# Output gates of two mixers, with tokens in rows and ahead of the transposition

## The chip, the cores and the metric

The kernel runs on one core of a Trainium2 chip. The metric is the device time of one launch in microseconds (us); the time of a kernel is the median over its runs. The engines that matter here: TensorE (PE) multiplies matrices, VectorE (DVE) and ScalarE (ACT) work elementwise, GpSimd (POOL) computes the few reciprocal roots of the norms, and SyncE (SP) issues the transfers from memory. Each engine works through its own queue in order.

## The reference

Two layers of a block for 256 tokens of 2048 columns, in float32. A projection `w_in` gives the inputs of three mixers: a convolution over time, HGRN (a gated linear recurrence, 6 heads of 128) and retention (6 heads of 128). HGRN and retention normalize the output of each head and multiply it with a gate from the same projection. That part, cut to what the change touches:

```python
# hgrn2_mixer, o: (b, t, heads, 128)
o = o * lax.rsqrt(jnp.mean(jnp.square(o), axis=-1, keepdims=True) + LN_EPS)
return o.reshape(b, t, D_HGRN) * norm_g * jax.nn.sigmoid(g_in.astype(jnp.float32))
# retention_mixer
o = ((o - mu) * lax.rsqrt(var + LN_EPS)).reshape(b, t, D_RET) * gn_g + gn_b
return jax.nn.silu(g_in.astype(jnp.float32)) * o
# the layer
mix = jnp.concatenate([y_conv, y_hgrn, y_ret], axis=-1).astype(dtype)
h = jnp.einsum('bte,ed->btd', mix, w_out[l])
x = layer_norm(DEEPNORM_ALPHA * x + h, ln1_g[l], ln1_b[l]).astype(dtype)
```

Behind it come a feed-forward part (2048 to 8192 to 2048, squared ReLU) and a second layer norm.

## The kernel before

**Matmuls.** Each float32 weight is split into two parts, by ScalarE (`hi`, L289) and VectorE (`lo`, L292), and so is each activation, and a product is three matmuls of parts. A unit of weights is 128 x 1024; units go through three raw buffers and six split ones (`wp`). There are two forms:

- `xstat` (matmuls in `mmx`, L315): the activation is the stationary operand. A group gives 256 tokens x 512 columns with tokens in rows, as 96 matmuls of 512 columns, 12 to a unit of weights.
- `wstat` (L366 and L368): the weights are the stationary operand. A call gives 256 columns (one pair of heads) with tokens along the free side, as 2 blocks of 16 pairs of matmuls, one 512 and one 256 wide, 8 pairs to a unit. Each block is evicted by a ScalarE copy (L375) and a VectorE sum (L378).

**The mixer stage of a layer.** `ORDER` lists the `wstat` calls. Three `xstat` groups `vgroup` give the values of HGRN and retention, the first ahead of the list, the others before ("hf", 2) and ("rq", 0). `hgrn` and `ret` do one pair of heads: TensorE computes scores in small float32 matmuls (HGRN: a diagonal, L591, and seven levels, L607, between which VectorE multiplies decays into both sides, L626 and L631; retention: L720, L721), then `out_heads` (L551 to L555) gives the heads' output with tokens in rows. VectorE takes the statistics (L530, L532), GpSimd the root, ScalarE scales (L667, L764), TensorE transposes (`transpose4`, L402), and only then, with channels in partitions, come the norm's factors (`hng`, `rgg`, `rgb`, a scalar for each partition), the gate from `wstat` (kinds "hg" and "rg"), and the split into `mixT` by `split_act` (L391, L393). The output projection `wo`, four `xstat` groups, reads `mixT`; the last quarter of its inputs are retention's pairs 1 and 2.

**What sets the order.** A planner (`Plan`) takes every operation with a cost and its dependences, and writes each engine's instructions in order of its own modelled times; TensorE's large matmuls (`main`) keep the program's order, the small ones and the other engines' work are put between them. The order is fixed when the program is built. Buffers come from rings: `r2` (11 of 128 x 512), `r1` (4 of 128 x 256), `mm` and `aux` (4 PSUM banks each).

Of the kernel before, what the change touches and what calls it, by code (L numbers as in the profile page):

```python
# [28 lines left out]
HP = 3  # L29


ORDER = [("cg", 0), ("ca", 0), ("hf", 0), ("hq", 0), ("hg", 0), ("cg", 1), ("ca", 1),
         ("hf", 1), ("hq", 1), ("hg", 1), ("hf", 2), ("hq", 2), ("hg", 2),
         ("rq", 0), ("rk", 0), ("rg", 0), ("rq", 1), ("rk", 1), ("rq", 2), ("rk", 2),
         ("rg", 1), ("rg", 2)]

MIXK = ((4, 8), (0, 4), (12, 4))
MT = (2, 0, 1, 3)
# [162 lines left out]
def block_kernel(ctx: ExitStack, tc: tile.TileContext, a: dict, out: bass.AP):  # L201
# [24 lines left out]
    def act(n, ptr=0, ps=False):  # L226
        return 0.000833 * n + (0.051 if ps else 0.093) + 0.093 * ptr
# [11 lines left out]
        C[name_] = cst.t[:, o_:o_ + n_]  # L239
        o_ += n_  # L240
    ident, tri = C["ident"], C["tri"]
    hng = C["hng"].rearrange("p (l n) -> p l n", l=2)
    rgg = C["rgg"].rearrange("p (l n) -> p l n", l=2)
    rgb = C["rgb"].rearrange("p (l n) -> p l n", l=2)
    clg = C["clg"].rearrange("p (l n) -> p l n", l=2)
    clb = C["clb"].rearrange("p (l n) -> p l n", l=2)
    cbd = C["cbd"].rearrange("p (l n) -> p l n", l=2)
# [149 lines left out]
    def transpose4(src, r, **kw):  # L397
        pt = aux.buf()

        def fn():  # L400
            for i in range(4):
                nc.tensor.transpose(out=pt.t[:, i * P:(i + 1) * P], in_=src()[:, i * P:(i + 1) * P], identity=ident)  # L402
# [138 lines left out]
    def out_heads(units, r, vt, col0):  # L541
# [16 lines left out]
        op("PE", 6 * 0.216, fn, r=r + vb, w=[po])  # L558
        return po

    def hgrn_gates(l, p, pr, pair):

        Tt, Kt = pv(pair, 0), pv(pair, 1)
        op("ACT", act(W), lambda: S.activation(out=Tt(), in_=pr.t, func=AF.Sigmoid), r=[pr], w=[(pair, "T")])
        op("ACT", act(W), lambda: S.activation(out=Kt(), in_=pr.t, func=AF.Sigmoid, scale=-1.0), r=[pr],
           w=[(pair, "K")])
        if l:
            for h in range(2):
                c = 2 * p + h
# [13 lines left out]
    def hgrn(l, p, pair, gate, vt, mixT):  # L583
# [78 lines left out]
        op("POOL", POW, lambda: rsqrt(s.t[:, 32:36], s.t, 40, 4), r=[mhalf], w=[s])  # L662
        on = r2.buf()

        def scale():
            for b in range(4):
                S.activation(out=on.t[:, b * P:(b + 1) * P], in_=po.t[:, b * P:(b + 1) * P], func=AF.Copy,  # L667
                             scale=s.t[:, 40 + b:41 + b])

        op("ACT", 4 * act(P, 1, True), scale, r=[po, s], w=[on])  # L670
        pt = transpose4(lambda: on.t, [on, cst])
        y = r2.buf()

        def gated():
            for h in range(2):
                c, sl = 2 * p + h, slice(h * T, (h + 1) * T)
                V.scalar_tensor_tensor(out=y.t[:, sl], in0=pt.t[:, sl], scalar=hng[:, l, c:c + 1],
                                       in1=gate.t[:, sl], op0=ALU.mult, op1=ALU.mult)
# [29 lines left out]
    def ret(l, p, pair, gate, vt, mixT):  # L708
# [59 lines left out]
        pt = transpose4(lambda: on.t, [on, cst])
        y = r2.buf()

        def affine():
            for h in range(2):
                c, sl = 2 * p + h, slice(h * T, (h + 1) * T)
                S.activation(out=y.t[:, sl], in_=pt.t[:, sl], func=AF.Identity, scale=rgg[:, l, c:c + 1],
                             bias=rgb[:, l, c:c + 1])

        op("ACT", 2 * act(T, 2, True), affine, r=[pt, cst], w=[y])
        op("DVE", dve(W), lambda: V.tensor_tensor(out=y.t, in0=y.t, in1=gate.t, op=ALU.mult), r=[gate], w=[y])
        blk = 10 + 2 * p
        mt, o = mixT[MT[blk // 4]], blk % 4  # L780
        split_act(mt, slice(o, o + 2), slice(0, T), lambda: y.t, [y], ("o", o))
# [167 lines left out]
    for l in range(DEPTH):  # L949
# [22 lines left out]
        else:  # L972
            vgroup(0, head=HEAD)
            norm.rest()
        pairs, gates = {}, {}
        for i, (kind, p) in enumerate(ORDER):
            if (kind, p) == ("hf", 2):
                vgroup(1)
            if (kind, p) == ("rq", 0):
                vgroup(2)  # L980
            if kind in ("hf", "rq"):
                pair = pairbufs.buf()
                pairs[kind[0], p] = pair
            dst = None
            if kind in ("rq", "rk"):
                dst = (pairs["r", p], "Q" if kind == "rq" else "K", pv(pairs["r", p], 0 if kind == "rq" else 1))
            pr = wstat(a["wp"][l, i], xT, dst)
            if l == 0 and i == 1:
                op("DMA", 6.0, lambda: nc.sync.dma_start(out=x_nat.t, in_=a["x"].rearrange("(t p) d -> p t d", p=P)),
                   w=[x_nat], after=(plan.last["PE"],))  # L990
            if kind == "hf":
                hgrn_gates(l, p, pr, pair)
            elif kind == "hq":
                Qv = pv(pair, 2)
                op("ACT", act(W), lambda Qv=Qv, pr=pr: S.activation(out=Qv(), in_=pr.t, func=AF.Sigmoid), r=[pr],
                   w=[(pair, "Q")])
                op("DVE", dve(W), lambda Qv=Qv, pr=pr: V.tensor_tensor(out=Qv(), in0=pr.t, in1=Qv(), op=ALU.mult),
                   r=[pr], w=[(pair, "Q")])
            elif kind == "hg":
                gate = r2.buf()  # L1000
                op("ACT", act(W), lambda gate=gate, pr=pr: S.activation(out=gate.t, in_=pr.t, func=AF.Sigmoid),
                   r=[pr], w=[gate])
                hgrn(l, p, pairs["h", p], gate, vt, mixT)
            elif kind in ("cg", "ca"):
# [15 lines left out]
            elif kind == "rg":  # L1020
                gate = r2.buf()
                op("ACT", act(W), lambda gate=gate, pr=pr: S.activation(out=gate.t, in_=pr.t, func=AF.Sigmoid),
                   r=[pr], w=[gate])
                op("DVE", dve(W), lambda gate=gate, pr=pr: V.tensor_tensor(out=gate.t, in0=pr.t, in1=gate.t,
                                                                           op=ALU.mult), r=[pr], w=[gate])
                ret(l, p, pairs["r", p], gate, vt, mixT)
# [76 lines left out]
def _columns():  # L1103

    start, off = {}, 0
    for name, n in (("ca", 512), ("cg", 512), ("hq", 768), ("hf", 768), ("hi", 768), ("hg", 768),
                    ("rq", 768), ("rk", 768), ("rv", 768), ("rg", 768)):
        start[name] = off
        off += n
    v = np.concatenate([start["hi"] + np.arange(768), start["rv"] + np.arange(768)])  # L1110
    blocks = []
    for kind, p in ORDER:
        base = start[kind] + 256 * p
        blocks.append(base + np.arange(256))
    return v, np.concatenate(blocks)
# [65 lines left out]
```

## Time and profile before

| | us |
|---|---|
| median of 3 runs | 2332.24 |
| lowest and highest run | 2331.98, 2335.85 |
| the profiled execution | 2335.01 |
| its span | 2333.2 |

Where layer 0's mixer stage lies in the span: TensorE starts its first stationary-weight stage at 33.2 us and the output projection at 363.9 us; layer 1's output projection starts at 1521.9 us. The granted TensorE clock was 0.998 over the run. In the profile's answers a group of instructions is named by line, engine, operation, and output<-input by the names in the program without buffer numbers; a row of the chain of waits is the start, the length, and what. The rows themselves stand in the prediction.

### The profile page before, as it was taken

To read this page: it belongs to the slowest core of one execution; us is meant where nothing else is said; L and a number is where in the kernel's file an instruction comes from. 1 tells how busy PE (TensorE), PEld (TensorE's weight loads), DVE (VectorE), ACT (ScalarE), POOL (GpSimd) and SP (SyncE) were. 2 spreads that over 40 slices of the span, in tenths; PEclk is the share of its full clock that TensorE was granted. 3 is DMA by queue.
4 is the path that set the end of the run, shared out by engine and by line. 5 is a ranking of instruction groups with operands and counts; after the bars stand their busy time and mean duration, and the time that the engine had idled before them with its cause. 6 is when DMAs were issued, how large, how long until landed. Compare 5 with 4: busy or idle time off the path is not lost.

```text
span 2333.2 us, 29611 instructions
## 1 busy us (share of the span) xinstructions
PE 2318.7 (99%) x12067; PEld 1975.0 (85%) x12067; DVE 1502.6 (64%) x2052; ACT 1050.9 (45%) x1334; POOL 47.9 (2%) x60
## 2 busy tenths in 40 slices
PE   9999999999999999999999999999999999999998
PEld 7888888888888888888888888888888888888886
DVE  6998565665565565565679976657655655655655
ACT  6445444454344344344444455444444444443442
POOL 0000000000000000000000000100000000000000
PEclk9999999999999999999999999999999999999999
DMA  8544556465555555556554445564655555555563
GB/s 291 183 169 163 172 194 212 163 208 189 189 189 190 199 181 193 188 189 205 208 173 161 163 163 177 184 219 171 204 192 196 184 194 186 190 188 198 181 230 113
DMA packets 67705, 439.90 MB, mean 189 GB/s; under 512 B 7664, under 2 KB 7920, under 8 KB 16624
## 3 DMA queue, kind: packets, MB, share of 16 engines
q1 hardware_dynamic: 67568, 438.01, 54.7%
q8 instruction: 94, 1.54, 0.2%
q14 instruction: 43, 0.35, 0.0%
HBM read 432.74 MB, written 2.10 MB: 186 GB/s over the span
## 4 chain that ended last, share of the span: by engine, by line
PE 98%; ACT 1%; DVE 0%; DMA 0%; issue 0%; SPq 0%; DVEq 0%
PE mm L315 44%; PE mm L366 33%; PE mm L368 17%; PE aux L607 2%; PE aux L402 1%; DMA raw<-in_wv 0%; DVE wp L292 0%; PE aux L555 0%; ACT act L391 0%; PE aux L553 0%; PE aux L591 0%; PE aux L551 0%; PE aux L720 0%; ACT wp L289 0%; ACT r L916 0%; PE aux L648 0%
## 5 line engine op out<-in xcount | busy, mean ns | idle before, releaser
L292 DVE TENSOR_TENSOR wp<-raw,wp 128x1024 fp32r<-128x1024 f32 (+1 forms) x786 | 957.5, 1221 | 580.3 <-ACT wp L289 578.7
L366 PE MATMUL mm<-act,wp 128*128 128x512 f32 x3328 | 1180.6, 399 | 0.0
L289 ACT CAST wp<-raw 128x1024 fp32r<-128x1024 f32 (+1 forms) x786 | 825.2, 1052 | 771.8 <-PE mm L315 505.1
L315 PE MATMUL mm<-wp,act 128*128 128x512 f32 x4416 | 1019.4, 391 | 3.0 <-ACT wp L289 1.6
L315 PEld LDWEIGHTS mm<-wp,act 128*128 128x128 f32 x4416 | 825.9, 188 | 176.5 <-DVE wp L292 3.7
L368 PE MATMUL mm<-act,wp 128*128 128x256 f32 x3328 | 933.0, 280 | 0.0
L366 PEld LDWEIGHTS mm<-act,wp 128*128 128x128 f32 x3328 | 625.4, 188 | 151.4
L368 PEld LDWEIGHTS mm<-act,wp 128*128 128x128 f32 x3328 | 628.3, 189 | 0.5
L375 ACT COPY r<-mm 128x256 f32<-128x256 f32 x208 | 77.8, 374 | 371.0 <-PE mm L368 370.6
L378 DVE TENSOR_TENSOR r<-mm,r 128x256 f32<-128x256 f32 x184 | 78.0, 424 | 147.0 <-ACT r L375 146.6
L794 DVE SCALAR_TENSOR_TENSOR r<-u_t,cst,r 128x256 f32<-128x256 f32 x240 | 102.2, 480 | 0.0
L410 POOL TENSOR_TENSOR sm<-sm,mhalf 128x4 f32<-128x4 f32 (+1 forms) x24 | 28.3, 1181 | 2275.8 <-DVE sm L876 1611.7
L391 ACT CAST act<-r 128x512 fp32r<-128x512 f32 x82 | 51.7, 631 | 21.6 <-DVE r L1052 16.1
L393 DVE TENSOR_TENSOR act<-r,act 128x512 fp32r<-128x512 f32 x82 | 56.2, 685 | 0.0
L315 PE MATMUL mm<-act,act 128*128 128x512 f32 x192 | 44.8, 389 | 0.0
L607 PEld LDWEIGHTS aux<-pair 128*128 128x128 f32 x336 | 42.4, 191 | 2.6
L943 DVE TENSOR_TENSOR x_nat<-x_nat,mm 128x512 f32<-128x512 f32 x48 | 31.0, 682 | 18.8 <-PE mm L315 18.7
L1052 DVE SCALAR_TENSOR_TENSOR r<-r 128x512 f32<-128x512 f32 x60 | 41.6, 693 | 2.1
L315 PEld LDWEIGHTS mm<-act,act 128*128 128x128 f32 x192 | 36.0, 188 | 7.5
L607 PE MATMUL aux<-pair 128*128 128x64 f32 x336 | 42.0, 267 | 0.0
L941 DVE SCALAR_TENSOR_TENSOR x_nat<-x_nat,mm 128x512 f32<-128x512 f32 x32 | 20.8, 682 | 13.0 <-PE mm L315 13.0
L896 ACT ACTIVATE x_nat<-x_nat,sm 128x512 f32<-128x512 f32 x6 | 4.9, 817 | 48.1 <-POOL sm L416 48.1
(118 smaller groups left out, 576.4 us busy)
## 6 DMA issues: line engine op xcount, KB each, us to landing
raw<-in_w SPq DMA_DIRECT2D x248, 1024.0 KB, 4.8
raw<-in_wp SPq DMA_DIRECT2D x88, 1024.0 KB, 4.8
raw<-in_wo SPq DMA_DIRECT2D x32, 1024.0 KB, 4.8
raw<-in_wv SPq DMA_DIRECT2D x20, 1024.0 KB, 4.8
raw<-in_w1x SPq DMA_DIRECT2D x8, 1024.0 KB, 5.3
raw<-in_wv SPq DMA_DIRECT2D x6, 512.0 KB, 5.9
pair<-pair SPq DMA_DIRECT2D x24, 128.0 KB, 2.3
x_nat<-in_x SPq DMA_DIRECT2D x1, 2048.0 KB, 9.5
```

The costliest lines, as they stand in the source:

```text
L289: S.copy(out=wt()[:, 0, sl], in_=raw.t[:, rs])
L292: V.tensor_tensor(out=wt()[:, 1, sl], in0=raw.t[:, rs], in1=wt()[:, 0, sl].bitcast(F32), op=ALU.subtract)
L315: nc.tensor.matmul(ps.t, lhsT=xT[k // 4].t[:, xs, k % 4, t * P:(t + 1) * P], rhs=w[:, ws, kb, :], start=(k == 0 and n == 0), stop=(k == KB ...
L366: nc.tensor.matmul(pv, lhsT=w[:, 0, kb, :], rhs=xt[:, :, k % 4, :], start=(k == 0), stop=False)
L368: nc.tensor.matmul(pv[:, 0, :], lhsT=w[:, 1, kb, :], rhs=xt[:, 0, k % 4, :], start=False, stop=(k == KB - 1))
L375: S.copy(out=low.t, in_=ps.t[:, T:])
L378: V.tensor_tensor(out=dst[2]()[:, b * T:(b + 1) * T], in0=ps.t[:, 0:T], in1=low.t, op=ALU.add)
L391: op("ACT", act(n, ps=ps), lambda: S.copy(out=x.t[:, 0, blks, cols], in_=bl(src(), nb)), r=r, w=[(x, part)], **kw)
L393: op("DVE", dve(n), lambda: V.tensor_tensor(out=x.t[:, 1, blks, cols], in0=bl(src(), nb), in1=x.t[:, 0, blks, cols].bitcast(F32), op=ALU.s ...
L607: nc.tensor.matmul(ps.t[:, b * 64:(b + 1) * 64], lhsT=Kt()[:, b * P:(b + 1) * P], rhs=rhs, start=True, stop=True)
L794: V.scalar_tensor_tensor(out=d, in0=src, scalar=cw[:, l, b, j:j + 1], in1=d, op0=ALU.mult, op1=ALU.add)
L1052: op("DVE", dve(W), lambda f=f, r=r: V.scalar_tensor_tensor(out=f.t, in0=r.t, scalar=0.0, in1=r.t, op0=ALU.max, op1=ALU.mult), r=[r], w=[f ...
```

## The change

The gates of HGRN and retention leave the `wstat` list. Three `xstat` groups of 512 columns take their place (`out_gates`), each with two pairs of heads: HGRN 0 and 1, HGRN 2 and retention 0, retention 1 and 2. Gates now come with tokens in rows, like the heads' output. ScalarE's sigmoid reads PSUM directly (for retention VectorE multiplies with the gate's input), and the norm's factors, loaded as rows and broadcast to all partitions, are multiplied in on VectorE; for retention there are two products, the gate with the factor and the gate with the offset. HGRN's scaling and gating become one VectorE operation for each 128 columns; retention's scaled output is multiplied with the one product, and the other is added. The transposition comes after that, and `split_act` reads it from PSUM. A pair of heads starts when its projections and its gate have both been put into the program. Arrays of factors in `cst` (36 of 710 columns) fall away.

```diff
-ORDER = [("cg", 0), ("ca", 0), ("hf", 0), ("hq", 0), ("hg", 0), ("cg", 1), ("ca", 1),
-         ("hf", 1), ("hq", 1), ("hg", 1), ("hf", 2), ("hq", 2), ("hg", 2),
-         ("rq", 0), ("rk", 0), ("rg", 0), ("rq", 1), ("rk", 1), ("rq", 2), ("rk", 2),
-         ("rg", 1), ("rg", 2)]
+ORDER = [("cg", 0), ("ca", 0), ("hf", 0), ("hq", 0), ("gates", 0), ("cg", 1), ("ca", 1),
+         ("hf", 1), ("hq", 1), ("hf", 2), ("hq", 2), ("gates", 1),
+         ("rq", 0), ("rk", 0), ("rq", 1), ("rk", 1), ("rq", 2), ("rk", 2), ("gates", 2)]
+
+GATES = ((("h", 0), ("h", 1)), (("h", 2), ("r", 0)), (("r", 1), ("r", 2)))
...
+    def mixed(y, blk, mixT):
+        pt = transpose4(lambda: y.t, [y, cst])
+        mt, o = mixT[MT[blk // 4]], blk % 4
+        split_act(mt, slice(o, o + 2), slice(0, T), lambda: pt.t, [pt], ("o", o), ps=True)
+
+    def out_gates(l, n, xT):
+        res, after = [r2.buf(), r2.buf()], (plan.last["PE"],)
...
+        def done(t, ps):
+            for j, (kind, p) in enumerate(GATES[n]):
+                src = lambda j=j: bl(ps.t[:, j * T:(j + 1) * T], 2)
+                op("ACT", act(T, ps=True), lambda j=j, src=src: S.activation(
+                    out=view(res[j], t), in_=src(), func=AF.Sigmoid), r=[ps], w=[(res[j], t)], floor=1.5)
+                if kind == "r":
+                    op("DVE", dve(T), lambda j=j, src=src: V.tensor_tensor(
+                        out=view(res[j], t), in0=src(), in1=view(res[j], t), op=ALU.mult), r=[ps], w=[(res[j], t)],
+                       floor=1.5)
+
+        xstat(a["wv"][l, 3 + n], xT, done)
+        for j, (kind, p) in enumerate(GATES[n]):
+            rows = []
+            for name in ("hngr",) if kind == "h" else ("rgbr", "rggr"):
+                row = r1.buf()
+                rows.append(row)
+                op("DMA", 0.5, lambda row=row, name=name, p=p: nc.sync.dma_start(
+                    out=row.t, in_=a[name][l, p * T:(p + 1) * T].partition_broadcast(P)), w=[row], after=after)
+            add = None
+            if kind == "r":
+                add = r2.buf()
+
+            for row in rows:
+                dst = add if row is rows[0] and kind == "r" else res[j]
+                op("DVE", dve(W), lambda j=j, row=row, dst=dst: V.tensor_tensor(
+                    out=view(dst), in0=view(res[j]), in1=bl(row.t, 2).unsqueeze(2).broadcast_to([P, 2, 2, P]),
+                    op=ALU.mult), r=[row, res[j]], w=[dst])
+            yield (kind, p), (res[j] if kind == "h" else (res[j], add))
...
-        op("ACT", 4 * act(P, 1, True), scale, r=[po, s], w=[on])
-        pt = transpose4(lambda: on.t, [on, cst])
-        y = r2.buf()
-
-        def gated():
-            for h in range(2):
-                c, sl = 2 * p + h, slice(h * T, (h + 1) * T)
-                V.scalar_tensor_tensor(out=y.t[:, sl], in0=pt.t[:, sl], scalar=hng[:, l, c:c + 1],
+        def gated():
             for b in range(4):
+                sl = slice(b * P, (b + 1) * P)
+                V.scalar_tensor_tensor(out=on.t[:, sl], in0=po.t[:, sl], scalar=s.t[:, 40 + b:41 + b],
                                        in1=gate.t[:, sl], op0=ALU.mult, op1=ALU.mult)
 
-        op("DVE", 2 * dve(T, 1), gated, r=[pt, gate, cst], w=[y])
...
+        op("DVE", 4 * dve(P, 1), gated, r=[po, s, gate], w=[on])
+        mixed(on, 4 + 2 * p, mixT)
...
-        op("ACT", 2 * act(T, 2, True), affine, r=[pt, cst], w=[y])
-        op("DVE", dve(W), lambda: V.tensor_tensor(out=y.t, in0=y.t, in1=gate.t, op=ALU.mult), r=[gate], w=[y])
...
+        for g, o in zip(gate, (ALU.mult, ALU.add)):
+            op("DVE", dve(W), lambda g=g, o=o: V.tensor_tensor(out=on.t, in0=on.t, in1=g.t, op=o), r=[g], w=[on])
+        mixed(on, 10 + 2 * p, mixT)
...
+        def at_work(k, q):
+            ready.append((k, q))
+            if ready.count((k, q)) == 2:
+                (hgrn if k == "h" else ret)(l, q, pairs[k, q], gates[k, q], vt, mixT)
```

The planner's order moves with it. TensorE, layer 0, the scores of the first HGRN pair (`aux`, from `pair_70`): before, a level stands eight pairs of matmuls behind the one ahead of it, in the `wstat` stages that follow the pair's projections. Here the last pairs ahead of a level, and the level.

```order
L366 MATMUL mm_104<-act_74,wp_67 128x512
L368 MATMUL mm_104<-act_74,wp_67 128x256
L366 MATMUL mm_104<-act_74,wp_67 128x512
L368 MATMUL mm_104<-act_74,wp_67 128x256
L607 MATMUL aux_107<-pair_70 128x64 x4
L366 MATMUL mm_104<-act_75,wp_67 128x512
L368 MATMUL mm_104<-act_75,wp_67 128x256
```

Now the diagonal (L633) and the levels (L649) stand in the gates' own `xstat` stage (L313; `mm_103` and `mm_104` are its two halves of the tokens).

```order
L633 MATMUL aux_106<-pair_70 128x128 x4
L313 MATMUL mm_103<-wp_66,act_73 128x512 x6
L313 MATMUL mm_104<-wp_66,act_73 128x512 x6
L313 MATMUL mm_103<-wp_67,act_73 128x512 x6
L649 MATMUL aux_107<-pair_70 128x64 x4
L313 MATMUL mm_104<-wp_67,act_73 128x512 x6
L313 MATMUL mm_103<-wp_68,act_74 128x512 x6
L649 MATMUL aux_108<-pair_70 128x64 x4
```

Between two levels lie twelve `xstat` matmuls where eight pairs lay; five of the seven levels come in this stage, the other two in the `wstat` stage behind it.

TensorE, layer 0, the end of the stage: the last retention pair. Before, its transposition stood twelve pairs ahead of the output projection, in the last gate's stage.

```order
L366 MATMUL mm_102<-act_72,wp_66 128x512
L368 MATMUL mm_102<-act_72,wp_66 128x256
L402 MATMUL aux_106<-cst,r_4_84 128x128 x4
L366 MATMUL mm_102<-act_73,wp_66 128x512
L368 MATMUL mm_102<-act_73,wp_66 128x256
```

Now the transpositions of pairs 1 and 2 (L400) stand inside the first group of the output projection, which reads `act_76`, `act_78`, `act_77` and, for retention's pairs 1 and 2, `act_79`.

```order
L400 MATMUL aux_105<-cst,r_10_90 128x128 x4
L313 MATMUL mm_102<-wp_64,act_78 128x512 x6
L313 MATMUL mm_101<-wp_65,act_78 128x512 x6
L313 MATMUL mm_102<-wp_65,act_78 128x512 x6
L313 MATMUL mm_101<-wp_66,act_77 128x512 x6
L400 MATMUL aux_106<-cst,r_4_84 128x128 x4
L313 MATMUL mm_102<-wp_66,act_77 128x512 x6
L313 MATMUL mm_101<-wp_67,act_77 128x512 x6
L313 MATMUL mm_102<-wp_67,act_77 128x512 x6
L313 MATMUL mm_101<-wp_68,act_79 128x512 x6
```

From the last transposition to the first matmul that reads `act_79` there are now 18 matmuls.

VectorE at the same place: before, only the last gate (L1024, its input times its sigmoid), its product with the output (L778) and the output's split stood between the weights' splits.

```order
L292 TENSOR_TENSOR wp_67<-raw_61,wp_67 128x1024
L1024 TENSOR_TENSOR r_2_82<-r_7_87,r_2_82 128x512
L778 TENSOR_TENSOR r_3_83<-r_3_83,r_2_82 128x512
L292 TENSOR_TENSOR wp_68<-raw_62,wp_68 128x1024
L393 TENSOR_TENSOR act_79<-r_3_83,act_79 128x512
L292 TENSOR_TENSOR wp_69<-raw_62,wp_69 128x1024
```

Now both pairs' gates are finished there: the gate's input times its sigmoid (L580, from PSUM), the products with the rows (L598), and the first product into a head's output (L800).

```order
L580 TENSOR_TENSOR r_9_89<-mm_103,r_9_89 128x2x128
L580 TENSOR_TENSOR r_1_81<-mm_103,r_1_81 128x2x128
L580 TENSOR_TENSOR r_9_89<-mm_104,r_9_89 128x2x128
L580 TENSOR_TENSOR r_1_81<-mm_104,r_1_81 128x2x128
L598 TENSOR_TENSOR r_6_86<-r_9_89,r_1_92 128x512
L598 TENSOR_TENSOR r_0_80<-r_1_81,r_2_93 128x512
L598 TENSOR_TENSOR r_9_89<-r_9_89,r_0_91 128x512
L598 TENSOR_TENSOR r_1_81<-r_1_81,r_3_94 128x512
L290 TENSOR_TENSOR wp_67<-raw_61,wp_67 128x1024
L800 TENSOR_TENSOR r_10_90<-r_10_90,r_9_89 128x512
```

Eight instructions of the gates stand in one piece ahead of the next weights' split; the last six wait for the second half of the tokens.

More of the change, by code (lines that the diff above doesn't have):

```diff
@@ L42 @@
 HEAD, TAIL = 6, 6
-PACK = (("ident", P), ("tri", P), ("lbt", 12), ("hng", 12), ("rgg", 12), ("rgb", 12), ("clg", 8), ("clb", 8),
+PACK = (("ident", P), ("tri", P), ("lbt", 12), ("clg", 8), ("clb", 8),
         ("cbd", 8), ("cw", 8 * CONVW), ("inv", 1), ("sgn", 1), ("lng", 3 * KB), ("lnb", 3 * KB),
@@ L241, in block_kernel @@
     ident, tri = C["ident"], C["tri"]
-    hng = C["hng"].rearrange("p (l n) -> p l n", l=2)
-    rgg = C["rgg"].rearrange("p (l n) -> p l n", l=2)
-    rgb = C["rgb"].rearrange("p (l n) -> p l n", l=2)
     clg = C["clg"].rearrange("p (l n) -> p l n", l=2)
@@ L559, in out_heads, with view @@
         return po
+    def mixed(y, blk, mixT):
[4 more added lines that the diff above has]
+        res, after = [r2.buf(), r2.buf()], (plan.last["PE"],)
+        def view(b, t=None):
+            v = b.t.rearrange("p (h t e) -> p h t e", h=2, t=2)
+            return v if t is None else v[:, :, t, :]
+        def done(t, ps):
[24 more added lines that the diff above has]
+            yield (kind, p), (res[j] if kind == "h" else (res[j], add))
     def hgrn_gates(l, p, pr, pair):
@@ L663, in hgrn @@
         on = r2.buf()
-        def scale():
+        def gated():
             for b in range(4):
-                S.activation(out=on.t[:, b * P:(b + 1) * P], in_=po.t[:, b * P:(b + 1) * P], func=AF.Copy,
-                             scale=s.t[:, 40 + b:41 + b])
-        op("ACT", 4 * act(P, 1, True), scale, r=[po, s], w=[on])
-        pt = transpose4(lambda: on.t, [on, cst])
-        y = r2.buf()
-        def gated():
-            for h in range(2):
-                c, sl = 2 * p + h, slice(h * T, (h + 1) * T)
-                V.scalar_tensor_tensor(out=y.t[:, sl], in0=pt.t[:, sl], scalar=hng[:, l, c:c + 1],
+                sl = slice(b * P, (b + 1) * P)
+                V.scalar_tensor_tensor(out=on.t[:, sl], in0=po.t[:, sl], scalar=s.t[:, 40 + b:41 + b],
                                        in1=gate.t[:, sl], op0=ALU.mult, op1=ALU.mult)
-        op("DVE", 2 * dve(T, 1), gated, r=[pt, gate, cst], w=[y])
-        blk = 4 + 2 * p
-        mt, o = mixT[MT[blk // 4]], blk % 4
-        split_act(mt, slice(o, o + 2), slice(0, T), lambda: y.t, [y], ("o", o))
+        op("DVE", 4 * dve(P, 1), gated, r=[po, s, gate], w=[on])
+        mixed(on, 4 + 2 * p, mixT)
     def rotate(X, Y, pair):
@@ L767, in ret @@
         op("ACT", 4 * act(P, 2, True), scale, r=[po, s], w=[on])
[L768 to L775, printed above, removed]
-        op("ACT", 2 * act(T, 2, True), affine, r=[pt, cst], w=[y])
[L778 to L781, printed above, removed]
+        for g, o in zip(gate, (ALU.mult, ALU.add)):
+            op("DVE", dve(W), lambda g=g, o=o: V.tensor_tensor(out=on.t, in0=on.t, in1=g.t, op=o), r=[g], w=[on])
+        mixed(on, 10 + 2 * p, mixT)
     def conv_taps(l, acc, b0):
@@ L974, in block_kernel @@
             norm.rest()
-        pairs, gates = {}, {}
-        for i, (kind, p) in enumerate(ORDER):
+        pairs, gates, ready = {}, {}, []
+        def at_work(k, q):
+            ready.append((k, q))
+            if ready.count((k, q)) == 2:
+                (hgrn if k == "h" else ret)(l, q, pairs[k, q], gates[k, q], vt, mixT)
+        for i, (kind, p) in enumerate(ORDER):
+            if kind == "gates":
+                for (k, q), gate in out_gates(l, p, xT):
+                    gates[k, q] = gate
+                    at_work(k, q)
+                continue
             if (kind, p) == ("hf", 2):
@@ L986, in block_kernel @@
                 dst = (pairs["r", p], "Q" if kind == "rq" else "K", pv(pairs["r", p], 0 if kind == "rq" else 1))
-            pr = wstat(a["wp"][l, i], xT, dst)
+            pr = wstat(a["wp"][l, i - sum(k == "gates" for k, _ in ORDER[:i])], xT, dst)
             if l == 0 and i == 1:
@@ L998, in block_kernel @@
                    r=[pr], w=[(pair, "Q")])
[L999 to L1004, printed above, removed]
+            if kind in ("hq", "rk"):
+                at_work(kind[0], p)
+            if kind in ("cg", "ca"):
                 def uv(p=p):
@@ L1019, in block_kernel @@
                         conv(l, accs, mixT)
[L1020 to L1026, printed above, removed]
         for g in range(4):
@@ L1109, in _columns @@
         off += n
-    v = np.concatenate([start["hi"] + np.arange(768), start["rv"] + np.arange(768)])
+    v = np.concatenate([start["hi"] + np.arange(768), start["rv"] + np.arange(768)]
+                       + [start[k + "g"] + 256 * p + np.arange(256) for two in GATES for k, p in two])
     blocks = []
     for kind, p in ORDER:
+        if kind == "gates":
+            continue
         base = start[kind] + 256 * p
@@ L1154 @@
     a["lbt"] = pp(i["hgrn_lb"], 6)
-    a["hng"] = pp(i["hgrn_norm_g"], 6)
-    a["rgg"] = pp(i["ret_gn_g"], 6)
-    a["rgb"] = pp(i["ret_gn_b"], 6)
+    a["hngr"], a["rggr"], a["rgbr"] = i["hgrn_norm_g"], i["ret_gn_g"], i["ret_gn_b"]
     a["clg"] = pp(i["conv_ln_g"], 4)
```

## The prediction

> **What bounds the kernel now.** The page first: its busy shares and the chain that ended last.
>
> ```profile
> PE 2318.7 (99%) x12067; PEld 1975.0 (85%) x12067; DVE 1502.6 (64%) x2052; ACT 1050.9 (45%) x1334; POOL 47.9 (2%) x60
> ...
> PE 98%; ACT 1%; DVE 0%; DMA 0%; issue 0%; SPq 0%; DVEq 0%
> ```
>
> TensorE is busy for 2318.7 of 2333.2 us and the chain runs along it for 98%. A busy PE could still be waiting inside its stream, so next come the waits of PE and of its weight loads, and the windows of layer 0's mixer stage (columns: stretch, length, busy us of each engine, clock, DMA share, GB/s).
>
> ```profile
> PE mm L315 <- ACT wp L289: 1.6, 2, 1.2
> PE aux L452 <- DVE wz L447: 1.2, 1, 1.2
> PE mm L315 <- DVE wp L292: 1.0, 2, 0.8
> ...
> PEld aux L402 <- ACT r L764: 1.0, 5, 0.2
> ```
>
> ```profile
> 58.00:117.00 59.00, 59.00 (x363) 52.31 (x362) 56.22 (x115) 24.43 (x34) 0.00 (x0) 1.00 0.53 186
> 117.00:175.00 58.00, 58.00 (x341) 50.92 (x341) 56.00 (x118) 24.52 (x34) 1.86 (x1) 1.00 0.49 168
> ...
> 233.00:292.00 59.00, 59.00 (x329) 51.01 (x329) 34.91 (x64) 25.72 (x36) 1.55 (x2) 1.00 0.51 170
> 292.00:364.00 72.00, 71.98 (x426) 63.07 (x425) 48.47 (x80) 37.10 (x60) 8.44 (x12) 1.00 0.56 182
> ```
>
> Over the whole run PE waits under 4 us, and in the mixer stage not at all but for 1.0 us at transpositions. So the time is the sum of what PE issues: a change counts if it changes that sum or makes PE wait. VectorE is the engine that could make it wait: 112.2 of 117 us from 58 to 175, where the convolution's taps and the first two HGRN pairs lie; later it idles (83.4 of 131 us from 233 to 364).
>
> **Term 1: the gates' matmuls, -5.1 us.** A gate pair of 256 columns cost 32 pairs of matmuls (512 and 256 wide); now two of them share one `xstat` of 96 matmuls, 512 wide. The durations of single matmuls overlap, so the price is their spacing, from the chain of waits (start, length, what) in the feed-forward part, where `xstat` stages and eight `wstat` calls alternate with nothing between.
>
> ```profile
> 545.47 87.05 PE mm L315 x384
> 722.95 87.06 PE mm L315 x384
> 900.46 87.06 PE mm L315 x384
> ```
>
> 87.05 / 384 = 0.2267 us for a matmul of `xstat`. From 545.47 + 87.05 to 722.95 are 90.43 us for 8 x 32 = 256 pairs: 0.3532 a pair. So 512 gate columns cost 64 x 0.3532 = 22.61 us before and 96 x 0.2267 = 21.76 us after; 0.845 us saved, six times in two layers: **-5.07 us**.
>
> The Trainium skill (TensorE: Matmul & The Clock Gate, Back-to-back issue gap) gives N/2.4 + 2.5 ns from one matmul to the next, 0.2158 us for 512 columns and 0.1092 for 256. By that the pair costs 0.325, the gate group 20.80 us before and 20.72 after, and the term is an estimated -0.5 us. The rows disagree: the 256-wide matmul takes 0.3532 - 0.2267 = 0.1265 us. I go by the rows.
>
> **Term 2: small matmuls move into `xstat` stages, +1.5 us.** PE's order shows 36 of the 42 score groups (four 128x64 matmuls, L607) inside `xstat` stages where 20 were, and all six diagonal groups (L591) where none was. What such a group adds to PE depends on its neighbours. Starts of the first and the last of a run of groups, first among pairs (eight between two groups), then among `xstat` matmuls (twelve):
>
> ```profile
> 89.37 0.84 PE aux L607 x8
> 115.15 0.45 PE aux L648 x4
> ...
> 158.13 0.84 PE aux L607 x8
> 180.02 0.44 PE aux L648 x4
> ```
>
> Among pairs: 25.78 / 7 = 3.683, less 8 x 0.3532 = 2.826, leaves 0.857 us for a group. Among `xstat` matmuls: 21.89 / 6 = 3.648, less 12 x 0.2267 = 2.720, leaves 0.928. The move costs 0.071 us for a score group, 16 x 0.071 = 1.1 us. The diagonal groups are not to be seen inside an `xstat` stage; bounds are nothing and one group's whole 0.93 us, and I take the 0.071 of the nearest row, 0.4 us. Of the other small groups four more stand there than before, at nothing to 0.071 each. Sum **+1.5 us**.
>
> **Other engines, cover.** Means of the groups that go, stay or stand nearest to what is new:
>
> ```profile
> L375 ACT COPY r<-mm 128x256 f32<-128x256 f32 x208 | 77.8, 374 | 371.0 <-PE mm L368 370.6
> L378 DVE TENSOR_TENSOR r<-mm,r 128x256 f32<-128x256 f32 x184 | 78.0, 424 | 147.0 <-ACT r L375 146.6
> L667 ACT ACTIVATE r<-aux,sm 128x128 f32<-128x128 f32 x24 | 6.9, 373 | 0.0
> L726 DVE SCALAR_TENSOR_TENSOR r<-aux,cst 128x128 f32<-128x128 f32 x24 | 7.3, 345 | 4.6 <-PE aux L721 4.6
> L677 DVE SCALAR_TENSOR_TENSOR r<-aux,cst,r 128x256 f32<-128x256 f32 x12 | 5.2, 478 | 0.1
> L778 DVE TENSOR_TENSOR r<-r,r 128x512 f32<-128x512 f32 x6 | 4.1, 688 | 0.6 <-ACT r L774 0.5
> ```
>
> VectorE, an HGRN pair: two evictions (0.424) and two 256-wide gatings (0.478) go; a row product (0.688, like L778) and four 128-wide gatings (0.345, like L726) come: 2.07 against 1.80, +0.3 us. A retention pair: two evictions and two 512-wide products become two 256-wide and four 512-wide products: +1.4 us. That is +5 us a layer; the 0.6 us of the first two HGRN pairs lies in the stretch with 4.8 us idle, the rest where 47 us are idle. ScalarE loses the evictions, four 0.373 scalings or two affine steps a pair, and is at 45%. Neither is on the path unless an instruction that PE waits for stands behind them; I count nothing. The weights' split shows how far weights run ahead. This is VectorE's 31st unit of weights; PE, at the first pair's diagonal, has gone through 96 matmuls and 144 pairs, 8 + 18 = 26 units.
>
> ```profile
> 84.23 0.89 PE aux L591 x8
> ...
> 86.40 1.22 DVE L292 TENSOR_TENSOR wp<-raw,wp 128x1024 fp32r<-128x1024 f32 x1
> ```
>
> That is over four units of 2.7 us, some 11 us, so waits of VectorE for a gate's last matmul (new, with weights' splits queued behind) don't reach PE through the weights. If that cover were gone, each us of wait would be a us of time.
>
> **SP's queue.** Nine row loads of 128 KB a layer come in; SP waits for the start of the gate stage and a free `r1` buffer before it issues each. Ahead of them, the loads of that stage's weights are already out, and the rows are wanted only when it ends, 21.8 us later; the two 256 KB and 128 KB broadcasts of the page land in 6.0 and 7.6 us.
>
> ```profile
> r<-in_l1g SPq DMA_DIRECT2D x8, 256.0 KB, 6.0
> ...
> r<-in_pos SPq DMA_DIRECT2D x1, 128.0 KB, 7.6
> ```
>
> The last pair's `rotate` swap (K half) stands behind four of them. It can come some us late, and VectorE holds weights' splits meanwhile: inside the 11 us. Counted at nothing, at most 2 us.
>
> **Term 3: transpositions after the retention norm, +0.6 us.** This chain has no cover now. Pair 1 of layer 0, in order of time (the norm's statistics, POOL, scaling, transposition):
>
> ```profile
> 326.24 0.89 DVE L530 BATCH_NORM_STATS2 sm<-aux 128x6 f32<-128x128 f32 x4 [0.45 <-PE aux L555]
> ...
> 330.13 1.22 DVE L292 TENSOR_TENSOR wp<-raw,wp 128x1024 fp32r<-128x1024 f32 x1
> 330.35 1.06 POOL L756 TENSOR_TENSOR sm<-sm 128x4 f32<-128x4 f32 x1
> ...
> 332.08 1.50 ACT L764 ACTIVATE r<-aux,sm 128x128 f32<-128x128 f32 x4 [2.08 <-POOL sm L757]
> 332.98 0.98 PE L402 MATMUL aux<-cst,r 128*128 128x128 f32 x4
> ```
>
> From the statistics to the last scaled piece it is 7.3 us, and PE, which has 20 pairs (7.06 us) in between, is held a little inside the transpositions. The change puts two products (0.688 each, some 1.4 us) behind the scaling, and PE's order gives 24 pairs (8.48 us) for pair 0, and 36 `xstat` matmuls with a transposition (8.6 us) for pair 2: 1.4 us more for 1.4 us more. So about the same small wait, between nothing and 0.4 us for each of six; I add 0.1 us each, **+0.6 us**. For HGRN the four scalings (1.5 us) become four gatings (1.4 us) on VectorE: nothing. At the end of the stage pair 2's last transposition comes 18 matmuls (4.1 us) ahead of the output projection's use; after it come two 512-wide copies (0.6 and 0.7 us) and perhaps one weights' split (1.22): covered, by over 1 us.
>
> **Sum.** -5.07 + 1.5 + 0.6 = **-3.0 us**. The profiled execution took 2335.01 us, 1.8 us around its span and 2.8 us above the median of the runs; the difference is taken off the median, 2332.24: **2329.3 us**, 0.13% less.
>
> **Rivals.**
>
> - *All of the saving arrives*: small matmuls cost the same anywhere and waits stay as they are. For it: PE's few waits now. Against it: the two spacings above. 2332.2 - 5.1 = 2327.2 us, just over 0.2%.
> - *Later transpositions give it back.* L756 took 1.06 us above beside a weights' split; with no split beside it, it took 0.20:
>
> ```profile
> 293.26 0.20 POOL L756 TENSOR_TENSOR sm<-sm 128x4 f32<-128x4 f32 x1
> ```
>
> More 512-wide products beside more norms, each holding POOL for up to its 0.688 us, would hold six chains by up to 4.1 us: 2329.3 + 4.1 = 2333.4, or about no change. The Trainium skill (SBUF — State Buffer, Who interferes with whom) says that a VectorE instruction with two SBUF inputs contends with a GpSimd instruction that reads SBUF; the two durations of L756 agree, and the rule speaks against this change.
>
> - *The matmuls' spacing goes by columns alone*: 64 x (512 + 256) and 96 x 512 are both 49152 columns, so term 1 is nothing, and 2332.2 + 2.1 = 2334.3 us. The rule of the Trainium skill on the issue gap, above, is nearly of this kind. The spacing rows speak against it, so it has little chance.
> - *VectorE becomes the bound of the HGRN levels* (slower). PE's score of a level needs two products of VectorE after the score before. Their starts, first and fifth of a run:
>
> ```profile
> 94.38 0.42 DVE L626 TENSOR_TENSOR pair<-pair 128x256 f32<-128x256 f32 x1
> ...
> 109.46 0.42 DVE L626 TENSOR_TENSOR pair<-pair 128x256 f32<-128x256 f32 x1
> ```
>
> 15.08 / 4 = 3.77 us a level, no shorter than PE's 3.65 among twelve `xstat` matmuls, where PE now runs most levels of both pairs. From the point where VectorE has no lead left, each level waits the difference and what stands ahead in the queue; at 0.3 us for each of the 28 levels of two pairs in two layers it is 8.4 us: 2329.3 + 8.4 = 2337.7, slower by 0.23%. Against it: the second pair already goes through twelve-matmul levels at this load without a wait.
>
> **Chances.** Forecast 0.55 (2327.8 to 2331.0 by its bounds), all saved 0.17, given back 0.09, by columns 0.03, VectorE 0.16. A measurement of this kernel can tell 0.2% (4.7 us) from no change. Faster by more: the second case and 0.03 of the first, 0.20; slower by more: the last, 0.16; within: 0.64. The range runs from the second case to the third and fourth, 2326.8 to 2334.5 us, and leaves the last out.
>
> **What would show it.** Right: six stages of 96 `xstat` matmuls of 21.8 us and their small matmuls at 0.93; PE still without waits for ACT or DVE on weights; wait at L400 transpositions under 3 us in all. Wrong, if PE waits at the scores of the first two pairs (VectorE), at out-heads or transpositions by over 0.5 us each, or at the output projection's matmuls 72 to 96; or if feed-forward stages change their spacing, which nothing here touches.

## Result and profile after

| | us |
|---|---|
| before, median of 10 runs | 2333.70 (2331.98 to 2335.85) |
| after, median of 10 runs | 2339.74 (2337.73 to 2345.05) |
| after / before, 95% interval | 1.0030 (1.0022 to 1.0039) |
| the profiled execution of after, its span | 2338.02, 2336.2 |

The change makes the kernel 0.3% slower: 6.0 us by the medians, where 3.0 us less were forecast, and outside the range. The page of after first, busy shares and chain:

```profile
PE 2315.7 (99%) x11875; PEld 1965.5 (84%) x11875; DVE 1509.1 (65%) x2070; ACT 1032.1 (44%) x1286; POOL 50.5 (2%) x60
...
PE 96%; DMA 1%; DVE 1%; ACT 1%; issue 0%; SPq 0%; DVEq 0%; ACTq 0%
```

PE is busy for 3 us less than before, and yet the span is 3 us longer. The chain now leaves PE for a DMA, VectorE and ScalarE. The waits of PE, of its weight loads and of VectorE say where (total us, times, longest):

```profile
PE aux L751 <- DVE pair L736: 5.3, 2, 2.8
PE aux L400 <- DVE r L800: 1.7, 2, 0.9
...
PEld aux L751 <- DVE pair L736: 6.3, 3, 3.2
...
PEld aux L400 <- ACT wp L287: 2.3, 2, 1.2
...
DVE pair L727 <- DMA pair<-pair: 9.5, 4, 4.1
```

In before PE waits at no retention score, its weight loads wait 1.0 us at transpositions, and VectorE waits for a swap once, 0.9 us. L751 is the score of a retention pair, L736 the last step of `rotate`, L727 its first, and the DMA `pair<-pair` the swap of two halves of 64 partitions that `rotate` begins with. PE's wait there comes once a layer, and it is always at pair 2, the last. The chain of after at this place in layer 0 (start, length, what):

```profile
336.61 0.47 SPq L721
...
337.13 7.29 DMA pair<-pair
...
344.53 0.69 DVE pair L727
345.23 0.60 DVE pair L731
345.83 0.07 DVE wp L290
345.90 0.98 issue
346.88 0.70 DVE pair L736
...
347.62 0.70 PE aux L751 x2
```

The swap is on its way for 7.29 us, and behind it come three products, a weights' split between them, and the score. In layer 1 the same row reads `1496.89 6.98 DMA pair<-pair`.

In layer 1 the wait has a second cost. Behind it the granted clock is 0.50 (third column from the right), and from the first matmul of the score to the next `xstat` matmul the chain takes 2.93 us (1507.08 to 1510.01), where layer 0, behind a wait as long but with the clock at 1.00, takes 1.57 (347.62 to 349.19):

```profile
347.00:350.00 3.00, 2.38 (x13) 2.10 (x14) 2.83 (x6) 0.00 (x0) 0.00 (x0) 1.00 0.69 213
...
1507.00:1510.00 3.00, 2.92 (x9) 2.56 (x10) 1.77 (x4) 0.00 (x0) 0.00 (x0) 0.50 0.88 292
```

Of the ten runs of after, the two with the lowest mean granted clock, 0.996, were the longest, 2343.79 and 2345.05 us.

What SP issues around the swap in layer 0, in the timeline of before and of after:

```profile
336.08 0.33 SPq L266 DMA_DIRECT2D raw<-in_wo  x1
339.14 0.47 SPq L690 DMA_DIRECT2D pair<-pair  x1
339.66 0.59 SPq L691 DMA_DIRECT2D pair<-pair  x1
```

```profile
333.98 0.33 SPq L264 DMA_DIRECT2D raw<-in_wo  x1
334.37 0.42 SPq L590 DMA_DIRECT2D r<-in_rgbr  x1
334.88 0.38 SPq L590 DMA_DIRECT2D r<-in_rggr  x1
335.32 0.46 SPq L590 DMA_DIRECT2D r<-in_rgbr  x1
336.23 0.33 SPq L590 DMA_DIRECT2D r<-in_rggr  x1
336.61 0.47 SPq L721 DMA_DIRECT2D pair<-pair  x1
337.13 0.59 SPq L722 DMA_DIRECT2D pair<-pair  x1
337.98 0.37 SPq L264 DMA_DIRECT2D raw<-in_wo  x1
```

SP is not late by much: the K half is evicted at 335.77 + 0.42 us and the swap is issued at 336.61. What is new are the four row loads of the last gate stage, 512 KB issued in the 2.2 us ahead of it. Times from issue to landing of all swaps (min, median, max) were 2.2, 2.3, 3.4 us before and 2.2, 2.4, 7.5 after.

The windows of after show how busy the DMA engines are while the swap is under way (second column from the right, their mean busy share): 0.65 in its first 4 us, nearly full in the rest.

```profile
337.00:341.00 4.00, 4.00 (x19) 3.33 (x18) 2.17 (x2) 1.25 (x2) 0.00 (x0) 1.00 0.65 210
341.00:344.50 3.50, 3.50 (x17) 2.83 (x16) 0.00 (x0) 1.83 (x2) 0.00 (x0) 1.00 0.98 286
```

Start-up varies from run to run, so spans are a poor measure of a few us. A better one is the mixer stage, from the first `wstat` matmul (layer 0) or from the layer norm's transposition (x16, layer 1) to the next norm's. Timeline and chain, before and then after:

```profile
33.20 0.39 PE L366 MATMUL mm<-act,wp 128*128 128x512 f32 x1
...
448.26 1.75 PE aux L402 x16
...
1162.32 1.75 PE aux L402 x16
...
1606.23 1.75 PE aux L402 x16
```

```profile
30.69 0.39 PE L364 MATMUL mm<-act,wp 128*128 128x512 f32 x1
...
448.13 1.75 PE aux L400 x16
...
1162.23 1.75 PE aux L400 x16
...
1609.07 1.75 PE aux L400 x16
```

415.06 and 443.91 us before, 417.44 and 446.84 after: +2.4 and +2.9, together +5.3 us. The feed-forward part between them takes 714.1 us in both.

### The profile page after: what moved, and what is told of

It reads as the page before. It is cut to its first block, busy times and chain, and to the rows that moved or that the text cites. A ratio compares the mean times of both kernels' runs of the same rounds, so it can differ in the third digit from the quotient of the medians.

```text
span 2336.2 us, 29265 instructions
## 1 busy us (share of the span) xinstructions
PE 2315.7 (99%) x11875; PEld 1965.5 (84%) x11875; DVE 1509.1 (65%) x2070; ACT 1032.1 (44%) x1286; POOL 50.5 (2%) x60
## 4 chain that ended last, share of the span: by engine, by line
PE 96%; DMA 1%; DVE 1%; ACT 1%; issue 0%; SPq 0%; DVEq 0%; ACTq 0%
PE mm L313 48%; PE mm L364 29%; PE mm L366 15%; PE aux L649 2%; PE aux L400 1%; DMA pair<-pair 1%; DMA raw<-in_wv 0%; DVE wp L290 0%; PE aux L751 0%; ACT act L389 0%; DMA raw<-in_xt 0%; PE aux L551 0%; PE aux L553 0%; PE aux L633 0%; PE aux L549 0%
## 5 line engine op out<-in xcount | busy, mean ns | idle before, releaser
L313 PE MATMUL mm<-wp,act 128*128 128x512 f32 x4992 | 1156.4, 391 | 2.1 <-DVE wp L290 1.3
L313 PEld LDWEIGHTS mm<-wp,act 128*128 128x128 f32 x4992 | 930.9, 188 | 197.0 <-DVE wp L290 4.0
L364 PE MATMUL mm<-act,wp 128*128 128x512 f32 x2944 | 1043.3, 399 | 0.0
L366 PE MATMUL mm<-act,wp 128*128 128x256 f32 x2944 | 826.2, 281 | 0.0
L364 PEld LDWEIGHTS mm<-act,wp 128*128 128x128 f32 x2944 | 553.1, 188 | 134.8
L366 PEld LDWEIGHTS mm<-act,wp 128*128 128x128 f32 x2944 | 556.1, 189 | 0.6
L373 ACT COPY r<-mm 128x256 f32<-128x256 f32 x184 | 68.8, 374 | 322.3 <-PE mm L366 322.2
L376 DVE TENSOR_TENSOR r<-mm,r 128x256 f32<-128x256 f32 x160 | 67.9, 424 | 134.8 <-ACT r L373 134.2
L389 ACT CAST act<-r 128x512 fp32r<-128x512 f32 x70 | 44.1, 633 | 16.1 <-DVE r L1074 16.1
L391 DVE TENSOR_TENSOR act<-r,act 128x512 fp32r<-128x512 f32 x70 | 48.0, 685 | 0.0
L649 PEld LDWEIGHTS aux<-pair 128*128 128x128 f32 x336 | 43.5, 191 | 3.1
L313 PE MATMUL mm<-act,act 128*128 128x512 f32 x192 | 44.8, 389 | 0.0
L313 PEld LDWEIGHTS mm<-act,act 128*128 128x128 f32 x192 | 36.0, 188 | 7.5
L649 PE MATMUL aux<-pair 128*128 128x64 f32 x336 | 42.0, 267 | 0.0
L391 DVE TENSOR_TENSOR act<-aux,act 128x512 fp32r<-128x512 f32 x34 | 22.8, 686 | 12.5 <-ACT act L389 12.5
```

The lines of the kernel that those rows point to most:

```text
L313: nc.tensor.matmul(ps.t, lhsT=xT[k // 4].t[:, xs, k % 4, t * P:(t + 1) * P], rhs=w[:, ws, kb, :], start=(k == 0 and n == 0), stop=(k == KB ...
L364: nc.tensor.matmul(pv, lhsT=w[:, 0, kb, :], rhs=xt[:, :, k % 4, :], start=(k == 0), stop=False)
L366: nc.tensor.matmul(pv[:, 0, :], lhsT=w[:, 1, kb, :], rhs=xt[:, 0, k % 4, :], start=False, stop=(k == KB - 1))
L373: S.copy(out=low.t, in_=ps.t[:, T:])
L376: V.tensor_tensor(out=dst[2]()[:, b * T:(b + 1) * T], in0=ps.t[:, 0:T], in1=low.t, op=ALU.add)
L389: op("ACT", act(n, ps=ps), lambda: S.copy(out=x.t[:, 0, blks, cols], in_=bl(src(), nb)), r=r, w=[(x, part)], **kw)
```

## Experiments

Three groups, each on one chip beside the kernel before: the first four (before 2333.68 us), the next four (2333.36), the last two (2332.92). The leading theory is that the rows delay the swap and the swap delays the score; the rivals are SP's queue order, and the wait of a transposition in its place. Stage lengths below are measured as above, layer 0 and layer 1.

**Rows behind the swap** (`e1_rows_late`). In the last gate stage the rows wait for its 8th block of main matmuls.

```diff
+        start = len(plan.ops)
         xstat(a["wv"][l, 3 + n], xT, done)
+        if n == 2:
+            after = ([o for o in plan.ops[start:] if o.main is not None][7],)
```

> The four factor rows of the last gate stage wait for the eighth of its sixteen matmul blocks, so they are issued behind the last pair's swap. Theory (swap behind rows): the swap lands in 2.3 to 2.6 us instead of 7.3, TensorE's wait at the scores of retention pair 2 goes in both layers, about 3 us each, and the time is 2332 to 2334.5 us, within 0.1% of before. Rival (VectorE's new products hold TensorE): the rows come later, the products not earlier, so 2338 us or more. Rival (what TensorE issues is longer than the sum said): no wait to be taken away, 2338 us or more.

2332.76 us, ratio 0.9994 (0.9986 to 1.0003); stages 414.94 and 442.55. The last pair's swap lands in 3.1 us in layer 0 and 4.3 in layer 1, later than the 2.3 to 2.6 expected. The wait at the score is gone all the same, and 7.0 us of time with it. TensorE's order moved too: the score stands 36 matmuls into the gate stage instead of 42, so it wants the swap sooner, which would make the wait longer and not shorter. What stays is the transposition (L400, 1.8 us).

**The same rows from ScalarE's queue** (`e2_rows_act`).

```diff
-                op("DMA", 0.5, lambda row=row, name=name, p=p: nc.sync.dma_start(
+                op("DMA", 0.5, lambda row=row, name=name, p=p: (nc.scalar if n == 2 else nc.sync).dma_start(
```

> The four factor rows of the last gate stage are issued from ScalarE's queue, at the time they had, and the swap from SP's. If the swap is late because it stands behind the rows in one queue: it lands in under 3 us and the time is 2332 to 2335 us. If the rows hold the DMA engines themselves, whatever the queue: it lands in 6 us or more and the time stays at 2337 to 2340 us.

2339.91 us, 1.0029 (1.0018 to 1.0041), as after. ScalarE's queue now issues the rows, from 336.56 us on, and the swap behind none of them on SP's takes as long as ever (timeline, then chain):

```profile
336.56 0.38 ACTq L590 DMA_DIRECT2D r<-in_rgbr  x1
...
338.24 0.39 ACTq L590 DMA_DIRECT2D r<-in_rggr  x1
```

```profile
337.83 7.99 DMA pair<-pair
```

So the queue's order isn't it; the transfers delay each other. Nor is it how closely the next weights' load follows: SP issues that load 0.63 us behind the swap's second half here, as in before (0.64), against 0.26 in after. The Trainium skill (DMA: Bandwidth & Descriptors, Rules for kernel authors) says that two transfers share the same 16 engines whether one engine issues them or two; this run agrees.

**Four row loads added to before** (`e3_before_rows`); nothing reads them.

```diff
+    dead = keep("dead", [P, T])
...
+            if (kind, p) == ("rg", 1):
+                for c in range(4):
+                    op("DMA", 0.5, lambda c=c: nc.sync.dma_start(
+                        out=dead.t, in_=a["l1g"][l, c * T:(c + 1) * T].partition_broadcast(P)), w=[(dead, c)],
+                       after=(plan.last["PE"],))
```

> The kernel before, with four row loads of 128 KB that nobody reads, issued at the start of the second-last retention gate, ahead of the last pair's swap. Theory (swap behind rows): the swap lands in 6 to 7.5 us and TensorE waits 1.5 to 3 us at the scores of pair 2 in each layer: 2336 to 2340 us. Rivals (the loss is in the gates' form or in the products): nothing changes, 2332 to 2335 us.

2353.97 us, 1.0086 (1.0072 to 1.0100): far too much, and for another reason. All four go to one place, each waited for the one before it, and SP's queue stood:

```profile
337.35 11.04 SPq L990 DMA_DIRECT2D dead<-in_l1g  x4
```

The swap came about 9 us later than before, and swaps then took 3.8 us at most; PE waited 13.4 us at the scores of two layers, and behind each wait the granted clock was 0.50 (355.6 to 361 us, 1522 to 1528 us), which made the loss larger than the waits. That shows what a late swap costs, not what a row does to it.

**The same with four places** (`e5_before_rows4`).

```diff
+                dead = [r2.buf(), r2.buf()]
...
+                        out=dead[c // 2].t[:, c % 2 * T:(c % 2 + 1) * T],
```

> The kernel before with four row loads of 128 KB that nobody reads, each into a place of its own (two buffers of the ring), issued at the start of the gate of retention pair 1, ahead of the last swap; the order on TensorE and VectorE stays but for the last pair's scores, which come four pairs later. Theory (row transfers hold the swap's transfer): the swap lands in 6.5 to 8 us instead of 2.3, TensorE waits at those scores 0.5 to 2 us in each layer, and the time is 2334.5 to 2338 us. Rival (the late swap belongs to the gate stage, not to the rows): it lands in 2.3 to 3 us and the time stays at 2333 to 2334.5 us.

2333.43 us, 1.0003 (0.9994 to 1.0012): missed. The swap is slower (5.2 us at most, 3.4 before), but PE waits 0.2 us only. Rows beside the swap delay it in before too. That it cost nothing belongs to this run's order, in which the score comes four pairs, 1.4 us, later; before's own order was not tested with so slow a swap. Why it took 5 us here and 7 in after is open: here the four rows were issued 2.6 to 0.5 us ahead of the swap, in after the last of them directly ahead.

**Two rows ahead, two behind** (`e7_two_rows`).

```diff
+        start = len(plan.ops)
...
+        mid = ([o for o in plan.ops[start:] if o.main is not None][7],)
...
+                   after=mid if (n, j) == (2, 1) else after)
```

> The changed kernel with two of the four rows of the last stage ahead of the swap and two behind it. Theory (the swap's transfer shares the DMA engines with the rows' transfers): the swap lands between the two cases, 4 to 6 us, and the time lies between 2332.8 and 2337 us. Rival (any row ahead holds it for the whole time): 7 us or more, 2338 to 2341 us.

2334.67 us, 1.0005 (0.9996 to 1.0014): between the two. Landing 5.8 us at most, waits at the score 1.5 us in the two layers together. In after, a landing of 7.29 left a wait of 2.78, so the room is 4.5 us; 5.8 would make 1.3 in a layer, and the longest wait was 1.1.

**POOL's cost in the planner** (`e4_pool_cost`). GpSimd's steps were charged less than they take; raised, the planner puts the transpositions later.

```diff
-    POOLC, POW = 0.26, 1.5
+    POOLC, POW = 0.45, 1.9
```

> The changed kernel with the planner's price of GpSimd raised to what the trace shows (1.9 us for the power, 0.45 for each operation behind it), so that transpositions stand later on TensorE. Theory (transposition of retention pair 0 is 1 us early in each layer): the waits at L400 of 2 to 4 us in all go, the late swap stays: 2336.5 to 2338.5 us. If these waits were only taken from slack: 2339 to 2341 us.

2332.63 us, 0.9996 (0.9987 to 1.0005), under what was expected. The waits at L400 are gone, but that is not all. The swap takes as long as in after (7.68 us in layer 0), yet the score waits little, since the order now puts it 48 matmuls into the gate stage instead of 42, and no weights' split stands between the swap's products any more (2.2 us from landing to score, 3.2 in after):

```profile
PE aux L751 <- DVE pair L736: 1.5, 2, 0.8
```

So the wait can be taken away from either end: an earlier swap or a later score.

**Both** (`e6_late_and_price`: `e1_rows_late` and `e4_pool_cost` together).

> The changed kernel with both: the last stage's rows behind the swap, and the planner's price of GpSimd at 1.9 and 0.45 us. Theory (what TensorE issues is 3.5 us shorter than before, and the two waits are all that stood against it): no waits at the scores of pair 2 nor at L400, 2329 to 2331.5 us, faster than before by 0.1 to 0.2%. Rival (the gain of the first two trials comes from the same place, so that it does not add): 2332 to 2333.5 us.

2331.31 us, 0.9992 (0.9983 to 1.0001); stages 414.62 and 441.86. No wait at L751 and L400 is left, but the price moved the layer norms as well, and the weight loads behind their transposed splits now wait (2.1 us for VectorE's, L391, and 1.4 for ScalarE's, L389).

**The price alone on before** (`e8_before_price`).

> The kernel before with the planner's price of GpSimd at 1.9 and 0.45 us. If that price is worth only what TensorE waits at transpositions: the 1.0 us of waits at L402 goes, 2332.5 to 2333.7 us. If it is worth more (as the 7 us that it brought on the changed kernel): 2331 us or less.

2334.41 us, 1.0005 (0.9996 to 1.0014): nothing gained, and over the range expected. Here too weight loads wait at the norms' splits, 1.9 and 0.8 us; that this is the reason was not tested.

**The price for the retention norm alone**, on `e1_rows_late` (`e9_late_ret_price`) and on before (`e10_before_ret_price`).

```diff
-        op("POOL", POW + 3 * POOLC, rs, r=[cst, mhalf], w=[s])
+        op("POOL", POW + 3 * POOLC + 1.0, rs, r=[cst, mhalf], w=[s])
```

> After with the rows of the last gate stage loaded behind the swap, and with the POOL cost that the order charges raised by 1.0 us for the retention's normalisation alone (the layer norms keep their price). Theory (the loss was the late swap, and what of the saving is still missing is the wait of pair 0's transposition): no wait of PE at the scores (L751) and none at the transpositions of the retention (L400), the layer norms' splits undisturbed; mixer stages about 414.6 and 441.9 us as in the run with both prices raised, time 2329 to 2331.5, ratio to before near 0.9985. Rival (the order only moves the idle time to another consumer): as with the rows late alone, 2332.8, ratio 0.9994.

> Before with the POOL cost raised by 1.0 us for the retention's normalisation alone. Theory: the short wait at the transposition after the retention's norm (under 1 us a layer before) goes, nothing else moves: 0.5 to 1 us less, 2332.5 to 2333.5, ratio 0.9996 to 1.0. Rival (the price is worth as much here as on after, so that it isn't the change's own cost): 2331 or less, ratio under 0.9990.

2331.03 us, 0.9991 (0.9982 to 1.0000), and 2332.05 us, 0.9998 (0.9989 to 1.0007). The first lies in its range; the second came out 0.5 us under its own. In the first, PE's waits are these, all at weights or at the start (timeline and chain below them); its weight loads wait once at a score, 0.4 us:

```profile
PE aux L450 <- DVE wz L445: 1.2, 1, 1.2
PE mm L313 <- ACT wp L287: 0.9, 1, 0.9
PE mm L313 <- DVE wp L290: 0.8, 1, 0.8
```

```profile
30.90 0.39 PE L364 MATMUL mm<-act,wp 128*128 128x512 f32 x1
...
444.20 1.75 PE aux L400 x16
...
1158.32 1.75 PE aux L400 x16
...
1600.22 1.75 PE aux L400 x16
```

Stages 413.30 and 441.90: 3.8 us less than before. With its own waits taken away in the same manner, before has 414.29 and 443.22, so the change itself, without any new wait, is worth 2.3 us. By the medians it is 1.0 us between these two kernels, within what the intervals allow. `e9_late_ret_price` is the fastest of all, at the edge of what can be told from before.

## Why the prediction was wrong

The two traces also give the distance from each matmul's start to the next. Summed over the mixer stages of both layers, as excess over the prediction's spacings of 0.2267 us (`xstat`) and 0.1265 us (the 256-wide half of a pair), they make up the difference:

| term | predicted us | measured us |
|---|---|---|
| 1, gates' matmuls | -5.07 | -5.07 (at these spacings) |
| 2, small matmuls in `xstat` stages, and the spacing around them | +1.5 | +2.1 |
| 3, transpositions after the retention norm | +0.6 | +0.9 |
| the swap behind the rows | 0, at most 2 | +7.4 |
| sum | -3.0 | +5.3 |

The sum is that of the two stages above; by the ratio's interval the change costs 5.1 to 9.1 us, which holds it.

**Term 1: right in the `xstat` matmuls.** Their spacing is as it was (of the pairs', see term 2). The output projection's long run, in the chain of after, gives 72.13 / 318 = 0.2268 us:

```profile
376.00 72.13 PE mm L313 x318
```

The rival by which spacing goes by columns falls.

**Term 2: right in kind, sized too small.** In layer 0 of after the diagonal and the levels stand among `xstat` matmuls:

```profile
81.56 0.89 PE aux L633 x8
...
86.55 0.84 PE aux L649 x8
...
101.16 0.84 PE aux L649 x8
```

A level costs (101.16 - 86.55) / 4 - 12 x 0.2267 = 0.93 us, as said, and the diagonal 4.99 - 18 x 0.2267 = 0.91. The 26 groups that moved are as counted. What was misread is the price among pairs. Pairs do not all stand 0.3532 us apart: from one small group to the next they keep either 0.353 or 0.347, and it was 0.347 in five of the seven distances from which the prediction took 0.857. With their own spacing a level among pairs costs 0.89 us, so moving a group costs about 0.04, 0.9 us for all 26. Most of the rest is term 1 counted too high: in before 484 of the 1408 pairs of the mixer stages stand at 0.347, in after 332 of 1024, which from 0.3532 makes 2.8 and 1.8 us. So the list without those pairs saves 1.0 us less than 0.3532 for each says. Together it is 2.1 us in place of 1.5.

**Term 3: near in sum, wrong in place.** It was to be 0.1 us for each of six transpositions. Pairs 1 and 2 wait for nothing; pair 0 waits in each layer:

```profile
304.52 0.71 ACT r L795 x2
...
305.25 0.69 DVE r L800
305.94 0.34 DVE pair L376
306.28 0.61 DVE r L800
...
307.02 0.63 PE aux L400 x4
```

Between the two products stands an eviction, and from the statistics (297.83 us) to the end of the last product it is 9.1 us, against 24 pairs of matmuls, 8.5 us. "1.4 us more for 1.4 us more" left out that eviction. The waits come to 2.1 us, where before had 1.1. With the rows already behind the swap, the price took away this wait and 2.3 us of stage length (1.6 and 0.7).

**SP's queue: the step that failed.** The prediction saw that the last pair's swap stands behind four row loads, and asked what holds PE if it is late. It answered with the weights: VectorE holds their splits, and these run 11 us ahead. That held: PE's waits for weights didn't grow. But the score of that very pair stands behind the swap too, and its room is 4.5 us from issue to landing; the prediction's signs of being wrong name the scores of the first two pairs and not this one. Nor did I ask whether the swap itself would take longer: I counted its place in the queue, which costs 0.4 us, and not the transfers beside it, which cost 5. Both were in the page: the swaps' landing of 2.3 us, the rows' of 6 and more. And a us of wait was more than a us of time: over the two layers the last pair's score starts 5.6 us late, and it and the matmuls right behind it take 1.7 us more, most of that in layer 1 at the granted clock of 0.50 (the 0.1 us left of the 7.4 is at other pairs' scores). So the loss is shown by undoing it (`e1_rows_late`), and the queue's part excluded (`e2_rows_act`). Whether the swap would be as slow beside the rows with no weights' load under way was not tried; that the load comes closer behind it in after than in before is not the cause, since in `e2_rows_act` it does not.

**Rivals.** *VectorE as the bound of the HGRN levels* has no wait at L649 in after. It gave 2337.7, which is slower, as measured, but for a reason that did not occur. *Given back by later transpositions* has its 2 us, at pair 0 alone. *All saved* stays out of reach even without new waits, by term 2.

## What to carry to other kernels

A small transfer that a compute chain waits for can be held by rows broadcast at the same time, on whichever queue they are issued; ask of each new load not only who wants it but which transfers fly beside it. When an instruction may come late, follow every consumer behind it: the widest cover (weights, 11 us) says nothing of the narrowest (this pair's score, 4.5 us). And where a planner sets the order by modelled costs, a cost that is too low puts a consumer too early; raise it for the one step, since here raising it everywhere moved waits to the norms.

## What was not expected of the hardware

- Each half of a swap, 128 KB inside the core's memory, mostly landed in 2.2 to 2.4 us. With four broadcast rows of 128 KB each issued beside it or just ahead it took 6.0 to 8.0 (after, `e2_rows_act`, `e4_pool_cost`), and 4.6 to 5.2 in `e5_before_rows4`, although these rows come to half of one weights' load of 1 MB, and the other swaps of these runs, among such loads, landed in 2.2 to 4.5 us. Whether the number of packets or the bytes do it was not tried.
- The first 512-wide matmul behind a small float32 group delays the next by 0.088 us on the mean, in all 30 places of layer 1 of `e9_late_ret_price`, whichever group it is. Among pairs it is nearly as much: 0.314 us from the 512-wide matmul behind a group to the next, 0.235 elsewhere.
- Pairs have two spacings in the mixer stages, each kept from one small group to the next. In before the 72 pairs from 124.17 us in layer 0 stand 0.347 us apart, and the same 72 in layer 1, from 1281.59 us, 0.353. What decides it was not looked into.
- Behind a wait of 2.47 us in layer 1 of after the granted clock fell to 0.50 for 3.4 us; behind one of 2.78 us in layer 0 it stayed at 1.00.
